# Grouped-query keys of x in one run of 512 columns: score matmuls 512 wide in a two-layer hybrid mixer

## Chip, cores and metric

The kernel runs on one core of a Trainium2 chip. The metric is device time in microseconds (us) of one execution, lower is better. All matrix products are made on TensorE (PE in the profile); VectorE is DVE, ScalarE is ACT, GpSimd is POOL, SyncE's queue of transfers is SP or SPq.

## The reference

Two layers of a mixer over 512 tokens of x and 256 tokens of a context. Each layer has three branches (differential attention, grouped-query attention, a long convolution). The change touches the second:

```python
def _gqa_attend(q, k, v):
    scale = GQ_DIM ** -0.5
    def body(qb):
        s = jnp.einsum('bqgrd,bkgd->bgrqk', qb, k).astype(jnp.float32) * scale
        p = jax.nn.softmax(s, axis=-1).astype(v.dtype)
        return jnp.einsum('bgrqk,bkgd->bqgrd', p, v)
    return _sweep_queries(body, q)
...
        kg_all = jnp.concatenate([kg_c, _rope_2d(kg, tab_gq)], axis=1)
        vg_all = jnp.concatenate([vg_c, vg], axis=1)
```

There are 8 query heads of 128 in 2 groups (g), each group with one key and one value head. Queries of x see all 768 keys (512 of x, 256 of the context). In the first layer the queries of the context see the 256 context keys alone; the second layer has no context output.

## The kernel before

Every fp32 operand is kept as a high part and a low part, and every product is three matmuls (`mm3`, lines 137 to 140: high by high, high by low, low by high) that add up in PSUM. A matmul has 128 stationary columns (a weight load, PEld, goes ahead of each) and streams 128, 256 or 512 columns of the other operand.

Tokens are worked on in pairs of 128-token tiles: pairs 0 and 1 are x, pair 2 is the context. For each group g the loop at lines 920 to 936 projects a pair (`proj_tok`, 48 matmuls of 256 columns into a PSUM tile `pst` of pool `pj`, which has two buffers), copies its value half out (`vv`, lines 927 and 582), norms and rotates its key half (`norm_rope`: products with tables at lines 598 and 602 read the same PSUM tile, a reciprocal root follows at lines 164 to 176), transposes the keys into another PSUM tile (line 932) and copies them out as a high and a low half of one SBUF tile `kk`. The dictionary `kT` has one such pair of 256 columns for each pair of tokens. These four places (two groups in two layers) are called the K stages below.

`scores` (lines 616 to 620) makes the scores of 128 queries: for each of the three pairs of keys one `mm3`, 256 columns into a part of a PSUM tile `S` of two banks of 512 columns. `softmax` takes the row maximum (DVE, line 634), the exponential (ACT, line 637) and the reciprocal; `pv` transposes the result (line 648) and multiplies it with the values (lines 655 to 658). `scores` is called with all three pairs 32 times in each layer, and in the first layer 16 times with the context pair alone.

The differential attention has its own scores (`scores_c`, lines 622 to 630, tiles `kH`, `kL`, `qT`), which the change leaves as they are. Its keys are taken from a projection by `evac_k` (lines 1037 to 1048), and its rotation products are at lines 1057 and 1061.

Attention steps, projections and the convolution's steps are generators that the projections tick, so the program mixes them. Then a scheduler puts each engine's instructions in order, from when it reckons that each can start. Engines run their own queues in order, and wait for each other by semaphores. All tiles named `u` (`vv`, `kk`, `qh`, the convolution's `uTh`, and others) share one pool of 20 buffers of 512 fp32 columns, handed out in the order of the program.

Of the kernel before, what the change touches and what calls it, by code (L numbers as in the profile page):

```python
# [11 lines left out]
F32R = mybir.dt.float32r  # L12
# [8 lines left out]
L, LC, D = 512, 256, 1024  # L21
# [47 lines left out]
def hybrid_mixer(ctx: ExitStack, tc: tile.TileContext, a, out):  # L69
# [5 lines left out]
    up = ctx.enter_context(tc.tile_pool(name="up", bufs=20))  # L75
# [61 lines left out]
    def mm3(ps, sh, sl, mh, ml, first, last):  # L137
        i0 = PE.matmul(ps, sh, mh, start=first, stop=False)  # L138
        PE.matmul(ps, sh, ml, start=False, stop=False)  # L139
        return i0, PE.matmul(ps, sl, mh, start=False, stop=last)  # L140
# [390 lines left out]
    def wchunk(l, ch):  # L531
        return [wload(a["w_in"][l, ch, :, 4 * j:4 * j + 4]) for j in range(2)]

    def layer(l, hx, hc, late, first):
# [7 lines left out]
        def proj_tok(W, pair):  # L542
            bg.tick()
            att.tock()
            ps = pj.tile([128, 2, 256], F32, tag="pj", name="pst")
            for i in range(2):
                for k in range(8):
                    Wh, Wl = W[k // 4]
                    mm3(ps[:, i], stat(2 * pair + i, k, 0), stat(2 * pair + i, k, 1),
                        Wh[:, k % 4], Wl[:, k % 4], k == 0, k == 7)  # L550
            return ps
# [16 lines left out]
        def gates(W, b0):  # L568
            for mb in range(2):
                for isx in ([True, False] if full else [True]):  # L570
                    n = L if isx else LC
                    ps = proj_feat(W, mb, isx)
                    v = tp.tile([128, n], F32, tag="tp", name="gv")
                    ACT.activation(v, ps, AF.Copy)
                    t = tp.tile([128, n], F32, tag="tp", name="sg")
                    sigmoid_into(t, v)
                    DVE.tensor_tensor(out=t, in0=v, in1=t, op=ALU.mult)
                    SP.dma_start(gd[12 * l + b0 + mb][:, 0:512] if isx else gd[12 * l + b0 + mb][:, 512:768], t)

        def evac_split(dh, dl, ps):  # L580
            ACT.activation(dh, ps, AF.Copy)  # L581
            return DVE.tensor_tensor(out=dl, in0=ps, in1=dh.bitcast(F32), op=ALU.subtract)  # L582

        def norm_rope(ps, H, pair, tab):
            g, C, S = tab
            v = ps.rearrange("p t (h d) -> p t h d", d=128)
            t1 = tp.tile([128, 2, H, 128], F32, tag="tp", name="t1")
            sq = tp.tile([128, 2, H, 128], F32, tag="tp", name="sq")
            ACT.activation(sq, v, AF.Square)
            if pair == 2:  # L590
                gb = g.unsqueeze(1).to_broadcast([128, H, 128])
                for t in range(2):
                    DVE.tensor_tensor(out=t1[:, t], in0=v[:, t], in1=gb, op=ALU.mult)
            else:
                t2 = tp.tile([128, 2, H, 128], F32, tag="tp", name="t2")
                for t in range(2):
                    tt = 2 * pair + t
                    DVE.tensor_tensor(out=t1[:, t], in0=v[:, t],
                                      in1=C[:, tt].unsqueeze(1).to_broadcast([128, H, 128]), op=ALU.mult)
                    for h in range(2):  # L600
                        d, s = slice(64 * h, 64 * h + 64), slice(64 - 64 * h, 128 - 64 * h)
                        DVE.tensor_tensor(out=t2[:, t, :, d], in0=v[:, t, :, s],  # L602
                                          in1=S[:, tt, d].unsqueeze(1).to_broadcast([128, H, 64]), op=ALU.mult)
                POOL.tensor_tensor(out=t1, in0=t1, in1=t2, op=ALU.add)
            ss = small(2 * H)
            DVE.tensor_reduce(out=ss, in_=sq.rearrange("p t h d -> p (t h) d"), axis=AX.X, op=ALU.add)
            r = rsqrt_cols(ss, 2 * H, 1.0 / 128)
            f = t1.rearrange("p t h d -> p (t h) d")
            DVE.tensor_tensor(out=f, in0=f, in1=r.unsqueeze(2).to_broadcast([128, 2 * H, 128]), op=ALU.mult)
            return f  # L610
# [4 lines left out]

        def scores(qh, ql, kT, klist):
            S = pS.tile([128, 1024], F32, tag="S", name="S")
            for i, kp in enumerate(klist):
                mm3(S[:, i * 256:(i + 1) * 256], qh, ql, kT[kp][0], kT[kp][1], True, True)
            return S  # L620

        def scores_c(c, q, kT, klist, i):
# [297 lines left out]
        for g in range(2):  # L920
            W = wchunk(l, GQ_C[g]["kv"])
            kT, V = {}, {}
            for p in pairs:
                ps = proj_tok(W, p)
                vv = up.tile([128, 2, 2, 128], F32R, tag="u", name="vv")
                vh, vl = vv[:, 0], vv[:, 1]
                evac_split(vh, vl, ps[:, :, 128:256])
                V[p] = (vh, vl)
                kr = norm_rope(ps[:, :, 0:128], 1, p, tabs["k"])
                T = pS.tile([128, 256], F32, tag="S", name="pst")  # L930
                for t in range(2):
                    PE.transpose(T[:, t * 128:(t + 1) * 128], kr[:, t], ident)
                kk = up.tile([128, 2, 256], F32R, tag="u", name="kk")
                kh, kl = kk[:, 0], kk[:, 1]
                evac_split(kh, kl, T)
                kT[p] = (kh, kl)
            for c in range(2):
                W = wchunk(l, GQ_C[g]["q"][c])
                qT = {}
                for p in qpairs:  # L940
                    ps = proj_tok(W, p)
                    qr = norm_rope(ps, 2, p, tabs["q"])
                    T = pS.tile([128, 2, 256], F32, tag="S", name="pst")
                    for h in range(2):
                        for t in range(2):
                            PE.transpose(T[:, h, t * 128:(t + 1) * 128], qr[:, 2 * t + h], ident)
                    qh = up.tile([128, 2, 256], F32R, tag="u", name="qh")
                    ql = up.tile([128, 2, 256], F32R, tag="u", name="ql")
                    evac_split(qh, ql, T)
                    qT[p] = (qh, ql)  # L950
                W = wchunk(l, GQ_C[g]["gate"][c])
                gates(W, 4 * g + 2 * c)
                if g == 0 and c == 0:
                    bg.drain()
                    for gen in late:
                        slow.add(gen)
                att.add(gq_att(g, c, kT, V, qT))
                att.spread(2 * len(qpairs) + 1, nq + {(0, 0): -full, (0, 1): 3, (1, 0): 0, (1, 1): 1}[g, c])
# [51 lines left out]
        for pr in range(2):  # L1010
# [10 lines left out]
            for hh in range(2):  # L1021
# [4 lines left out]
                qT, kT = {}, {}  # L1026
# [23 lines left out]
                for p in (0, 1):  # L1050
                    ps = proj_tok(W, p)
                    v = ps.rearrange("p t (c d) -> p t c d", d=64)
# [33 lines left out]
        def ysplit(i, src, shape):  # L1086
            if i < 12:
                t = hp.tile([128, 2] + shape, F32R, tag="h", name="yT")
            elif i < 14:
                t = dt.tile([128, 2] + shape, F32R, tag="dt", name="yT")  # L1090
            elif shape[0] == 1:
                t = up.tile([128, 2] + shape, F32R, tag="u", name="yT")
            else:
                t = None
            if t is not None:
                h, lo = t[:, 0], t[:, 1]
            else:
                h, lo = [pool.tile([128] + shape, F32R, tag=tag, name="yT")
                         for pool, tag in spare.get(i, [(up, "u")] * 2)]
            ACT.activation(h, src, AF.Copy)  # L1100
            (POOL if i < 12 else DVE).tensor_tensor(out=lo, in0=src, in1=h.bitcast(F32), op=ALU.subtract)
            return h, lo
# [13 lines left out]
        for b in order[8:15]:  # L1116
# [4 lines left out]
            if full and (b % 2 == 1 or b == 10):  # L1121
# [4 lines left out]
                h, lo = ysplit(ny, t, [len(bs), 256])  # L1126
# [228 lines left out]
    bg.add(f0)  # L1355
    bg.add(filter_gen(0, "0c", 256, h, w4))
    hx, hc = layer(0, hx, hc, [mod_gen(cs)], {b: (W0[b], acc[b]) for b in range(2)})
    bg.add(filter_gen(1, "1x", 512, h, []))
    layer(1, hx, hc, [], {})


# [137 lines left out]
```

## Time and profile before

| | us |
|---|---|
| median of 3 runs | 1585.81 (1583.59 to 1588.69) |
| the profiled execution, its own time | 1585.86 |
| its span, first to last instruction | 1584.1 |
| PE busy | 1500.6 (95%) |
| PE weight loads busy | 1349.7 (85%) |
| DVE busy | 1128.4 (71%) |
| ACT busy | 828.7 (52%) |
| POOL busy | 404.5 (26%) |

The span is 1.8 us shorter than the execution's own time. A matmul's shown duration includes its way through the array, and the next one starts before it ends: the durations of a run of matmuls add up to more than the time they take, and what one costs is the distance from its start to the next one's start.

### The profile page before, as it was taken

What the parts mean: (1) busy time and instruction counts of PE and PEld (TensorE: products, weight loads), DVE (VectorE), ACT (ScalarE), POOL (GpSimd) and SP (SyncE); (2) the same over time, 40 slices, a digit from 0 to 9 for tenths busy, and PEclk for the clock granted to TensorE, in tenths of its full rate; (3) what the DMA queues carried; (4) which work ended last, traced back from release to release, by engine and by line L of the source; (5) the groups of instructions that cost most, each with busy time, mean ns of one, the idle gap of its engine ahead of it and who ended that gap; (6) DMA issues with size and microseconds to landing.
All of it is one profiled execution on the core that took longest, in us unless ns stands there. A gap on an engine that the chain in (4) does not pass through costs nothing. (4 is left out here: it accounts for less than half of the span.)

```text
span 1584.1 us, 27024 instructions
## 1 busy us (share of the span) xinstructions
PE 1500.6 (95%) x10166; PEld 1349.7 (85%) x10166; DVE 1128.4 (71%) x2168; ACT 828.7 (52%) x1611; POOL 404.5 (26%) x436
## 2 busy tenths in 40 slices
PE   5989999999999999998999999998999999898997
PEld 3768888999998989898888878888999998798885
DVE  6767777877767475877754588769887656768657
ACT  5544343555466465666653356324556555657633
POOL 0243433212222141212002124233322223214014
PEclk9999999999999999999999999999999999999999
DMA  9437666323425253315343444764422222116242
GB/s 347 140 121 252 213 206 202 121 88 110 150 94 158 94 157 121 114 48 183 117 141 132 137 142 154 244 210 143 139 64 88 87 97 87 57 48 209 60 157 80
DMA packets 102134, 218.30 MB, mean 138 GB/s; under 512 B 11377, under 2 KB 46131, under 8 KB 102004
## 3 DMA queue, kind: packets, MB, share of 16 engines
q1 hardware_dynamic: 91492, 180.14, 34.6%
q0 software_dynamic: 9936, 35.39, 7.2%
q8 instruction: 80, 1.31, 0.3%
q10 hardware_dynamic: 576, 1.05, 0.2%
q14 instruction: 50, 0.41, 0.1%
HBM read 176.02 MB, written 40.52 MB: 137 GB/s over the span
## 5 line engine op out<-in xcount | busy, mean ns | idle before, releaser
L138 PE MATMUL psf<-hT,wh 128*128 128x512 f32 (+1 forms) x768 | 269.4, 355 | 13.5 <-DVE kL L1045 7.2
L138 PE MATMUL pst<-wh,hT 128*128 128x256 f32 x960 | 275.7, 287 | 6.7 <-DVE t L602 6.3
L140 PE MATMUL pst<-wh,hT 128*128 128x256 f32 x960 | 274.9, 286 | 0.0
L139 PE MATMUL pst<-wl,hT 128*128 128x256 f32 x960 | 274.4, 286 | 0.0
L139 PE MATMUL psf<-hT,wh 128*128 128x512 f32 (+1 forms) x768 | 268.3, 350 | 0.0
L140 PE MATMUL psf<-hT,wl 128*128 128x512 f32 (+1 forms) x768 | 267.6, 349 | 0.0
L156 DVE TENSOR_TENSOR wl<-raw,wh 128x1024 fp32r<-128x1024 f32 x140 | 178.2, 1274 | 93.2 <-ACT wh L152 82.9
L152 ACT ACTIVATE wh<-raw 128x1024 fp32r<-128x1024 f32 x140 | 147.9, 1057 | 94.5 <-PE psf L139 42.9
L138 PEld LDWEIGHTS pst<-wh,hT 128*128 128x128 f32 x960 | 184.4, 192 | 12.7 <-issue 10.0
L637 ACT ACTIVATE P<-S,sa 128x768 f32<-128x768 f32 (+1 forms) x160 | 130.2, 814 | 111.8 <-DVE sa L634 63.5
L139 PEld LDWEIGHTS pst<-wl,hT 128*128 128x128 f32 x960 | 184.5, 192 | 1.2 <-issue 0.8
L140 PEld LDWEIGHTS pst<-wh,hT 128*128 128x128 f32 x960 | 184.6, 192 | 0.9 <-issue 0.8
L138 PEld LDWEIGHTS psf<-hT,wh 128*128 128x128 f32 x768 | 146.2, 191 | 34.9 <-ACT P L977 4.3
L139 PEld LDWEIGHTS psf<-hT,wh 128*128 128x128 f32 x768 | 146.8, 191 | 16.7 <-issue 0.4
L140 PEld LDWEIGHTS psf<-hT,wl 128*128 128x128 f32 x768 | 146.4, 191 | 16.9
L634 DVE TENSOR_REDUCE sa<-S 128x1 f32<-128x768 f32 (+1 forms) x160 | 134.6, 841 | 26.9 <-PE S L629 17.7
L582 DVE TENSOR_TENSOR pl<-T,ph 128x512 fp32r<-128x512 f32 x156 | 107.0, 686 | 43.2 <-ACT ph L581 40.5
L581 ACT ACTIVATE ph<-T 128x512 fp32r<-128x512 f32 x156 | 92.6, 593 | 74.9 <-PE T L648 74.0
L138 PE MATMUL px<-wh,yT 128*128 128x512 f32 x320 | 126.1, 399 | 4.8 <-ACT P L977 3.6
L139 PE MATMUL px<-wl,yT 128*128 128x512 f32 x320 | 126.2, 395 | 0.0
L140 PE MATMUL px<-wh,yT 128*128 128x512 f32 x320 | 125.9, 394 | 0.0
L892 POOL TENSOR_TENSOR P<-P,sa 128x768 f32<-128x768 f32 (+1 forms) x40 | 52.4, 1309 | 207.6 <-DVE sa L639 198.1
(301 smaller groups left out, 3410.1 us busy)
## 6 DMA issues: line engine op xcount, KB each, us to landing
raw<-in_w_in SPq DMA_DIRECT2D x104, 512.0 KB, 4.1
raw<-in_w_out SPq DMA_DIRECT2D x36, 512.0 KB, 3.9
adaw<-in_ada_w SPq DMA_DIRECT2D x32, 512.0 KB, 4.6
tab<-in_inv POOLq DMA_DIRECT2D x20, 512.0 KB, 4.7
tab<-in_fwd POOLq DMA_DIRECT2D x18, 512.0 KB, 4.8
adaw<-in_ada SPq DMA_DIRECT2D x16, 512.0 KB, 10.6
yT<-yx POOLq DMA_DIRECT2D x16, 512.0 KB, 6.9
gl<-gd SPq DMA_DIRECT2D x60, 128.0 KB, 2.4
```

Of the source, the lines that this page charges most:

```text
L138: i0 = PE.matmul(ps, sh, mh, start=first, stop=False)
L139: PE.matmul(ps, sh, ml, start=False, stop=False)
L140: return i0, PE.matmul(ps, sl, mh, start=False, stop=last)
L152: ACT.activation(hi, src, AF.Copy)
L156: last_lo[0] = e.tensor_tensor(out=lo, in0=src, in1=hi.bitcast(F32), op=ALU.subtract)
L581: ACT.activation(dh, ps, AF.Copy)
L582: return DVE.tensor_tensor(out=dl, in0=ps, in1=dh.bitcast(F32), op=ALU.subtract)
L634: DVE.tensor_reduce(out=nm, in_=S[:, :n], axis=AX.X, op=ALU.max, negate=True)
L637: ACT.activation(P[:, :n], S[:, :n], AF.Exp, bias=nm, accum_out=s)
L892: POOL.tensor_tensor(out=P[:, :n], in0=P[:, :n], in1=rs.to_broadcast([128, n]), op=ALU.mult)
```

## The change

`kT` gets two entries for each group: `kT[True]`, a high tile `kkh` and a low tile `kkl` of 512 columns with all keys of x, and `kT[False]`, a tile `kk` with the two halves of the context's keys as before. Both 512-wide tiles are taken at pair 0 and each is written in two halves, by pair 0 and by pair 1. `scores` makes one `mm3` of 512 columns into the first bank of `S` and one of 256 into the second, in place of three of 256. The number of SBUF tiles is the same (three in each K stage); two of them are taken at pair 0.

```diff
         def scores(qh, ql, kT, klist):
             S = pS.tile([128, 1024], F32, tag="S", name="S")
-            for i, kp in enumerate(klist):
-                mm3(S[:, i * 256:(i + 1) * 256], qh, ql, kT[kp][0], kT[kp][1], True, True)
+            for isx, lo in [(True, 0), (False, 512)] if len(klist) > 1 else [(False, 0)]:
+                mm3(S[:, lo:lo + (L if isx else LC)], qh, ql, kT[isx][0], kT[isx][1], True, True)
             return S
...
-                kk = up.tile([128, 2, 256], F32R, tag="u", name="kk")
-                kh, kl = kk[:, 0], kk[:, 1]
-                evac_split(kh, kl, T)
-                kT[p] = (kh, kl)
+                if p == 0:
+                    kT[True] = [up.tile([128, 512], F32R, tag="u", name=nm) for nm in ("kkh", "kkl")]
+                if p < 2:
+                    evac_split(*[v[:, p * 256:(p + 1) * 256] for v in kT[True]], T)
+                else:
+                    kk = up.tile([128, 2, 256], F32R, tag="u", name="kk")
+                    kT[False] = (kk[:, 0], kk[:, 1])
+                    evac_split(*kT[False], T)
```

The scheduler also puts other instructions in another order, from the first K stage on (the lines after the K stage are numbered 4 higher). Three places follow.

PE, the scores of the first 128 queries (tile `S`, first layer, group 0), before:

```order
L138 MATMUL S_3622<-kk_2905,qh_3215 128x256
L139 MATMUL S_3622<-kk_2905,qh_3215 128x256
L140 MATMUL S_3622<-kk_2905,ql_3216 128x256
L138 MATMUL S_3622<-kk_3002,qh_3215 128x256
L139 MATMUL S_3622<-kk_3002,qh_3215 128x256
L140 MATMUL S_3622<-kk_3002,ql_3216 128x256
L138 MATMUL S_3622<-kk_3094,qh_3215 128x256
L139 MATMUL S_3622<-kk_3094,qh_3215 128x256
L140 MATMUL S_3622<-kk_3094,ql_3216 128x256
```

The same scores on PE in the changed kernel:

```order
L138 MATMUL S_3622<-kkh_2905,qh_3215 128x512
L139 MATMUL S_3622<-kkl_2906,qh_3215 128x512
L140 MATMUL S_3622<-kkh_2905,ql_3216 128x512
L138 MATMUL S_3622<-kk_3094,qh_3215 128x256
L139 MATMUL S_3622<-kk_3094,qh_3215 128x256
L140 MATMUL S_3622<-kk_3094,ql_3216 128x256
```

Nine matmuls of 256 columns become three of 512 and three of 256. In the whole program the matmuls on `S` from these keys go from 624 to 432.

DVE, the K stage of the first layer's group 0, where pair 1's projection (`pst_2922`, in the changed kernel `pst_2923`) is read, before (`us` is the convolution's, `wl` the low part of weights, `vv_2971` pair 1's values):

```order
L582 TENSOR_TENSOR uTl_2919<-uT_2915,uTh_2918 128x256
L582 TENSOR_TENSOR vv_2971<-pst_2922,vv_2971 128x256
L156 TENSOR_TENSOR wl_3443<-raw_3440,wh_3442 128x1024
L598 TENSOR_TENSOR t1_2974<-pst_2922,Ck_2789 128x128
L602 TENSOR_TENSOR t2_2977<-pst_2922,Sk_2790 128x64 x2
L598 TENSOR_TENSOR t1_2974<-pst_2922,Ck_2789 128x128
L602 TENSOR_TENSOR t2_2977<-pst_2922,Sk_2790 128x64 x2
L606 TENSOR_REDUCE sm_2985<-sq_2975 128x2
L778 SCALAR_TENSOR_TENSOR us_2809<-yps_2604,rn0x_1280,us_2809 128x256 x2
```

The same stretch of DVE's queue in the changed kernel:

```order
L582 TENSOR_TENSOR uTl_2920<-uT_2916,uTh_2919 128x256
L156 TENSOR_TENSOR wl_3443<-raw_3440,wh_3442 128x1024
L582 TENSOR_TENSOR vv_2972<-pst_2923,vv_2972 128x256
L582 TENSOR_TENSOR vv_3069<-pst_3020,vv_3069 128x256
L778 SCALAR_TENSOR_TENSOR us_2809<-yps_2604,rn0x_1280,us_2809 128x256 x2
L598 TENSOR_TENSOR t1_2975<-pst_2923,Ck_2789 128x128
L602 TENSOR_TENSOR t2_2978<-pst_2923,Sk_2790 128x64 x2
L598 TENSOR_TENSOR t1_2975<-pst_2923,Ck_2789 128x128
L602 TENSOR_TENSOR t2_2978<-pst_2923,Sk_2790 128x64 x2
```

Pair 2's values (`vv_3069`) and the convolution's two `us` instructions now stand ahead of the last reads of pair 1's projection.

DVE, differential attention of the last head of the first layer, where the keys of pair 0 (`kL_9325`, in the changed kernel `kL_9229`) are read out of their projection, before:

```order
L1033 SCALAR_TENSOR_TENSOR qT_9320<-pst_9260,qT_9320 64x256 x2
L1057 TENSOR_TENSOR t1_9504<-pst_9455,cosD_990 128x512
L639 RECIPROCAL sa_9254<-sa_9252 128x1
L1061 TENSOR_TENSOR t2_9505<-pst_9455,sinD_992 128x8x32 x2
L976 TENSOR_TENSOR sa_9256<-sa_9254,nl0_973 128x1
L634 TENSOR_REDUCE sa_9340<-S_9333 128x1
L1045 TENSOR_TENSOR kL_9325<-pst_9260,kH_9324 64x256 x2
```

The same stretch of DVE's queue in the changed kernel:

```order
L1037 SCALAR_TENSOR_TENSOR qT_9224<-pst_9164,qT_9224 64x256 x2
L639 RECIPROCAL sa_9158<-sa_9156 128x1
L980 TENSOR_TENSOR sa_9160<-sa_9158,nl0_973 128x1
L1049 TENSOR_TENSOR kL_9229<-pst_9164,kH_9228 64x256 x2
L1050 CAST kH_9228<-kH_9228 64x256
L634 TENSOR_REDUCE sa_9244<-S_9237 128x1
L1061 TENSOR_TENSOR t1_9408<-pst_9359,cosD_990 128x512
L1065 TENSOR_TENSOR t2_9409<-pst_9359,sinD_992 128x8x32 x2
```

The read of the keys now stands ahead of the row maximum and of the other pair's rotation products.

## Rows read from the trace of the kernel before

**Rows 1.** The page, part 1: busy time, share and instructions.

```profile
PE 1500.6 (95%) x10166; PEld 1349.7 (85%) x10166; DVE 1128.4 (71%) x2168; ACT 828.7 (52%) x1611; POOL 404.5 (26%) x436
```

**Rows 2.** Busy time by stretch: bounds, length, PE, PEld, DVE, ACT, POOL, clock, DMA.

```profile
260.00:300.00 40.00, 36.57 (x274) 35.38 (x273) 33.70 (x87) 15.92 (x35) 13.25 (x11) 0.96 0.47 155
300.00:640.00 340.00, 338.09 (x2549) 309.14 (x2548) 228.70 (x485) 189.72 (x404) 79.21 (x89) 1.00 0.39 123
1130.00:1340.00 210.00, 207.13 (x1536) 196.65 (x1537) 150.65 (x300) 123.17 (x237) 51.22 (x54) 1.00 0.28 90
```

**Rows 3.** PE's groups by line and shape: busy us, mean ns of one, idle before.

```profile
L139 PE MATMUL psf<-hT,wh 128*128 128x512 f32 x448 | 177.0, 395 | 0.0
...
L138 PE MATMUL S<-kk,qh 128*128 128x256 f32 x208 | 61.4, 295 | 0.5 <-ACT P L637 0.5
```

**Rows 4.** Timeline of PE, the first 18 score matmuls and the next: start, duration.

```profile
309.85 0.28 PE L138 MATMUL S<-kk,qh 128*128 128x256 f32 x1
...
312.01 0.28 PE L138 MATMUL pst<-wh,hT 128*128 128x256 f32 x1
```

**Rows 5.** Timeline of PE, 13 matmuls of 512 columns, first and last.

```profile
301.06 0.39 PE L140 MATMUL psf<-hT,wl 128*128 128x512 f32 x1
...
303.79 0.39 PE L140 MATMUL psf<-hT,wl 128*128 128x512 f32 x1
```

**Rows 6.** Timeline of the K stage, first layer, group 0, all engines.

```profile
263.21 0.28 PE L140 MATMUL pst<-wh,hT 128*128 128x256 f32 x1
...
263.41 1.06 ACT L152 ACTIVATE wh<-raw 128x1024 fp32r<-128x1024 f32 x1
...
263.96 0.42 DVE L582 TENSOR_TENSOR uTl<-uT,uTh 128x256 fp32r<-128x256 f32 x1
...
264.30 0.42 DVE L582 TENSOR_TENSOR vv<-pst,vv 128x256 fp32r<-128x256 f32 x1
264.63 1.22 DVE L156 TENSOR_TENSOR wl<-raw,wh 128x1024 fp32r<-128x1024 f32 x1
264.69 2.58 POOL L773 TENSOR_SCALAR us<-us,cols 128x512 f32<-128x512 f32 x1 [2.24 <-DMA us<-hyu]
...
265.76 0.28 DVE L598 TENSOR_TENSOR t<-pst,Ck 128x128 f32<-128x128 f32 x1
...
266.42 0.34 DVE L602 TENSOR_TENSOR t<-pst,Sk 128x64 f32<-128x64 f32 x2
...
266.91 0.39 PE L138 MATMUL pst<-wh,hT 128*128 128x256 f32 x1 [3.43 <-DVE t L602]
...
267.31 0.88 DVE L778 SCALAR_TENSOR_TENSOR us<-yps,rn0x,us 128x256 f32<-128x256 f32 x2 [0.22 <-POOL us L773]
```

**Rows 7.** Timeline of PE: two other long waits.

```profile
745.28 0.55 PE L138 MATMUL psf<-hT,wh 128*128 128x256 f32 x1 [4.15 <-DVE kL L1045]
...
1074.08 0.35 PE L138 MATMUL pst<-wh,hT 128*128 128x256 f32 x1 [2.85 <-DVE t L602]
```

**Rows 8.** Timeline of DVE and ACT ahead of the wait that ends at 745.28.

```profile
739.64 0.69 DVE L1057 TENSOR_TENSOR t<-pst,cosD 128x512 f32<-128x512 f32 x1
739.82 0.60 ACT L1042 ACTIVATE kH<-pst 128x512 fp32r<-128x512 f32 x1
740.32 0.73 DVE L1061 TENSOR_TENSOR t<-pst,sinD 128x256 f32<-128x256 f32 x2
740.97 2.53 DVE L976 TENSOR_TENSOR sa<-sa,nl 128x1 f32<-128x1 f32 x1
743.42 0.94 DVE L634 TENSOR_REDUCE sa<-S 128x1 f32<-128x768 f32 x1
744.29 0.84 DVE L1045 TENSOR_TENSOR kL<-pst,kH 64x256 fp32r<-64x256 f32 x2
```

**Rows 9.** Busy time by stretch, right behind two of the waits; the clock follows POOL.

```profile
267.10:270.50 3.40, 3.40 (x17) 3.40 (x17) 3.16 (x8) 1.04 (x3) 1.67 (x3) 0.50 0.54 186
745.00:748.40 3.40, 3.12 (x15) 3.15 (x15) 3.08 (x6) 1.71 (x4) 0.00 (x0) 0.50 1.13 418
```

## The prediction

> **What bounds the kernel now.** I read the page's busy line first [rows 1]: PE is busy for 95% of the span, DVE for 71%, so what the change saves on PE should count, unless it falls into a wait. The table by stretch says where: between 300 and 640 us and between 1130 and 1340 us, where nearly all the scores of grouped-query attention are made, PE is busy 338.09 of 340 us and 207.13 of 210 us [rows 2]. There is no idle time there for a saving to vanish in. In the K stage between 260 and 300 us PE is busy 36.57 of 40 [rows 2], and one wait explains that: 3.43 us, ended by DVE's last read of a projection [rows 6].
>
> The groups by line come next, and they are easily misread. A matmul of 512 columns is shown with a mean of 395 ns, one of 256 columns with 295 [rows 3]. From these, two narrow ones made into one would save about 195 ns. But shown durations overlap, and what counts is the distance between starts. The timeline shows 18 score matmuls of 256 columns from 309.85 to 312.01 [rows 4]: 2.16 us, 120 ns each. It shows twelve distances of 512-column matmuls from 301.06 to 303.79 [rows 5]: 2.73 us, 227 ns each. So 256 more columns cost 227 - 120 = 107 ns, and a matmul has 120 - 107 = 13 ns that do not depend on its columns.
>
> **Term 1, fewer matmuls.** 64 calls of `scores` with all keys (32 in each layer) lose three matmuls each: 624 become 432, 192 fewer, with the same number of columns. Each pair merged saves 2 x 120 - 227 = 13 ns on PE: 192 x 13 = 2.5 us. The weight loads that go with them (also 192 fewer) are already hidden, since 120 ns is the distance with one load for each matmul. Bounds: 0, if the 13 ns were columns after all, and 192 x 120 = 23.0 us, if the second half of a wide matmul cost nothing. Twelve equal distances of 227 ns put it at 13 ns.
>
> The Trainium skill (TensorE: Matmul & The Clock Gate, Back-to-back issue gap) gives two other figures. Its formula for a lone matmul has a fixed cost of 2.5 ns; by that the sum would have 192 x 2.5 = 0.5 us here in place of 2.5. Its sustained figure for 512 columns is about 131 ns, by which 192 x (240 - 131) = 20.9 us would go, an estimate from that page. This case's timeline agrees with neither: 13 ns and 227 ns [rows 4, 5].
>
> DVE's row maximum, ACT's exponential, the transposes, the bytes of keys copied out and all DMAs are the same in number and size. The two copies of each pair's keys go into halves of other tiles, at no cost. The first scores stand at 309.85 [rows 4], long after the K stage's copies, so waiting for both halves delays nothing; without that cover a copy of 0.42 us, like that of `vv` [rows 6], would show in each K stage.
>
> **Term 2, the K stage of the first layer.** The 20 `u` buffers are handed out in program order. Two buffers for keys are now taken at pair 0, so pair 2's values no longer stand behind pair 1's keys, and DVE gets them earlier: ahead of its last reads of pair 1's projection. PE waits for just these reads at 266.91, because the next projection needs that PSUM buffer [rows 6]. I replay DVE's new order with the durations of before. `uTl` ends at 264.38 (263.96 + 0.42). Then `wl` (1.22) ends at 265.60, two copies of values (0.42 each) at 266.44. The two `us` instructions now stand next; they need POOL's product, which ends at 264.69 + 2.58 = 267.27, and take 0.88: 268.15. The reads of the projection took from 265.76 to 266.76 (266.42 + 0.34), 1.00 us: 269.15. PE started 0.15 us after the last one and now would at 269.30: 2.4 us later. Queued behind these on DVE is the rest of pair 1's rotation, and for that PE waits only after another 48 matmuls (5.8 us at 120 ns). ACT's copy of the weights from 263.41 to 264.47 [rows 6] is moved ahead of pair 1's values, which DVE reaches later still. The SP and POOL queues have the same order up to here, so the transfer that POOL waits for is not moved. Bounds: 0, if POOL has its input 2.4 us sooner or DVE is earlier by another wait that shortens, and 4.0 us: the 2.4, and the clock. Right behind this wait the granted clock is 0.50 for 3.4 us [rows 9], the lower of TensorE's two levels, 1.2 in place of 2.4 GHz: in 745.00 to 748.40, after the other such wait, 15 matmuls of 256 columns ran, where 28 would fit at 120 ns, so such a stretch costs 13 x 120 ns = 1.6 us. A longer wait could bring a second one. I take 2.4, since the reads' order leaves the `us` instructions no way round.
>
> **Term 3, the last head of the first layer.** PE waits 4.15 us up to 745.28 for DVE's read of the keys `kL` [rows 7]. Ahead of it on DVE stand a 128x1 product of 2.53 us, stretched while POOL works, and a row maximum of 0.94 [rows 8]. In the new order the row maximum and the other pair's two rotation products (0.69 and 0.73) stand behind `kL`; so do, with the latter, the POOL additions that need them. Bounds: 0.94, the row maximum alone, and 4.15 + 1.6 = 5.8, the whole wait with the slow stretch after it [rows 9]; ACT's copy `kH` is there at 740.42 [rows 8], so `kL` could be. What is late next is the other pair's rotation, by 0.69 + 0.73 = 1.4 us, and PE's transposes wait for it. I take 4.15 - 1.4 = 2.7 us.
>
> Elsewhere the scheduler moves instructions by a few places on all engines, and waits shrink and grow. I find no side for that and take 0, with some 3 us to either side: about the size of one wait like that at 1074.08 [rows 7].
>
> **Sum**, against the profiled execution's own 1585.86 us (the median of three runs is 1585.81, the same): 1585.86 - 2.5 + 2.4 - 2.7 = 1583.1 us, 0.2% faster. About 0.3% (4.8 us) is what a measurement of this kernel can tell from no change.
>
> **Rivals.**
> - *Faster: the waits go too.* Term 3 at its far end (5.8), term 2 at 0: 1585.86 - 2.5 - 5.8 = 1577.6. For it: a wait of over 3 us with a slow clock behind it is worth more than the whole of term 1, and the new order undoes its cause at 745. Against: the same order lengthens the one at 266.91.
> - *Slower: values ahead of rotation.* In each of the four K stages DVE takes pair 2's values before pair 1's or the queries' rotation products, and PE waits for a PSUM buffer: 4 x 2.4 = 9.6, and the wait before 1074.08, of 2.85 us, behind which the first matmul took 0.35 us and not 0.55 as at 745.28 [rows 7], becomes long enough for one slow stretch: 1585.86 - 2.5 + 9.6 + 1.6 = 1594.6. It decides from (4.8 + 2.5) / 4 = 1.8 us for each stage. Against: the second group's stages showed no such wait before, with other work for PE to do, and the second layer's first has no `us` instruction in that place.
> - *Only columns count.* The change saves no PE time at all; terms 2 and 3 alone: 1585.86 + 2.4 - 2.7 = 1585.6. Against: 227 is not 240.
> - *Wide matmuls overlap.* The far end of term 1: 1585.86 - 23.0 + 2.4 - 2.7 = 1562.6. Against: [rows 5]. The page's 131 ns would give 1564.7, an estimate; the trace disagrees.
>
> **How the numbers follow.** Forecast (1583.1, within 0.3%) 0.50; only columns 0.05, also within; the waits go 0.31; wide matmuls overlap 0.01; slower 0.13. That is faster 0.32, same 0.55, slower 0.13. The forecast's own range is 3 us to either side for the moved waits and 1.6 for a slow stretch: 1578.5 to 1587.7. The range that should hold 8 in 10 reaches down to the faster rival, 1577, and up to where two of the four K stages are longer by 2.4 with a slow stretch and without term 3: 1585.86 - 2.5 + 4.8 + 1.6 = 1589.8, so 1590. What is left out is most of the slower rival and a tail of the faster one.
>
> **What would show it.** Term 1: 64 matmuls of 512 columns on `S` from each line of `mm3`, 227 ns from start to start, and a pair of score blocks taking 6 x 227 + 6 x 120 ns = 2.08 us in place of 2.16. Term 2: PE's wait near 267 us at 5 to 6 us, ended again by line 602. Term 3: the wait near 740 us ended by `kL` under 2 us. Wrong it would be if PE's idle time in the K stages or in differential attention changed by more than 3 us in a direction not named here, or if wide score matmuls stood further apart than 227 ns.

## The result and the profile after

The changed kernel takes 1596.35 us (median of 6 runs, 1595.01 to 1599.08); the kernel before took 1587.57 us beside it (6 runs). The ratio is 1.0054 with a 95% interval of 1.0041 to 1.0068: 0.5% slower, some 8.6 us. The forecast was 0.2% faster, with a range that ended at 1590. The profiled execution took 1599.08 us, with a span of 1597.0.

The page's busy line after, to be read beside [rows 1]:

```profile
PE 1508.8 (94%) x9974; PEld 1348.1 (84%) x9974; DVE 1120.5 (70%) x2168; ACT 826.1 (52%) x1611; POOL 406.1 (25%) x436
```

192 matmuls and weight loads are gone, as counted. The same three stretches as in [rows 2]:

```profile
260.00:300.00 40.00, 34.70 (x260) 34.01 (x259) 32.80 (x83) 14.13 (x32) 13.92 (x12) 0.91 0.43 135
300.00:640.00 340.00, 338.22 (x2458) 306.59 (x2457) 227.56 (x489) 188.50 (x401) 78.48 (x88) 1.00 0.38 121
1130.00:1340.00 210.00, 207.25 (x1439) 191.93 (x1438) 149.06 (x301) 120.20 (x231) 53.81 (x51) 1.00 0.28 91
```

In the two long stretches PE is as full as it was. In the K stage it lost 1.87 us of work (36.57 to 34.70), and the granted clock fell from 0.96 to 0.91.

PE's timeline of a pair of score blocks, first matmuls of each and the one behind them (for [rows 4]):

```profile
315.39 0.40 PE L138 MATMUL S<-kkh,qh 128*128 128x512 f32 x1
...
316.44 0.40 PE L138 MATMUL S<-kkh,qh 128*128 128x512 f32 x1
...
317.49 0.28 PE L138 MATMUL pst<-wh,hT 128*128 128x256 f32 x1
```

A pair takes 317.49 - 315.39 = 2.10 us in place of 2.16; 2.08 was forecast. The medians of the distances behind the 64 wide score matmuls of each line are 234, 232 and 229 ns for lines 138, 139 and 140, a little over the 227 of [rows 5]. Term 1 is there, at 32 x 0.06 = 1.9 us.

The K stage of the first layer, all engines, for [rows 6]:

```profile
264.36 1.06 ACT L152 ACTIVATE wh<-raw 128x1024 fp32r<-128x1024 f32 x1 [0.98 <-PE pst L139]
...
265.45 1.23 DVE L156 TENSOR_TENSOR wl<-raw,wh 128x1024 fp32r<-128x1024 f32 x1 [1.75 <-ACT wh L152]
...
266.20 1.05 ACT L152 ACTIVATE wh<-raw 128x1024 fp32r<-128x1024 f32 x1
...
267.15 0.65 ACT L581 ACTIVATE vv<-pst 128x256 fp32r<-128x256 f32 x2
267.28 1.62 DVE L156 TENSOR_TENSOR wl<-raw,wh 128x1024 fp32r<-128x1024 f32 x1 [0.27 <-ACT wh L152]
268.82 0.74 DVE L582 TENSOR_TENSOR vv<-pst,vv 128x256 fp32r<-128x256 f32 x2
269.27 0.76 ACT L589 ACTIVATE sq<-pst 128x256 f32<-128x256 f32 x2 [1.47 <-DVE vv L582]
269.49 0.86 DVE L778 SCALAR_TENSOR_TENSOR us<-yps,rn0x,us 128x256 f32<-128x256 f32 x2
...
270.93 0.34 DVE L602 TENSOR_TENSOR t<-pst,Sk 128x64 f32<-128x64 f32 x2
...
271.42 0.55 PE L138 MATMUL pst<-wh,hT 128*128 128x256 f32 x1 [5.30 <-DVE t L602]
```

The wait of 3.43 us has become 5.30, ended by line 602 as forecast. The reader should follow the chain backward: the reads stand behind both `us`, these behind two copies of values, and those behind the split of the weights, which waits for ACT's `wh`. ACT copies the values (267.15) behind `wh` (266.20), where it did so ahead of it before.

The end of the first layer, all engines, where the wait of 4.15 us for `kL` stood [rows 7, 8]:

```profile
753.52 0.68 DVE L1105 TENSOR_TENSOR yT<-yld,yT 128x512 fp32r<-128x512 f32 x1
...
754.22 0.80 SPq L1122 DMA_DIRECT2D yld<-yx  x2
...
757.78 0.63 ACT L1104 ACTIVATE yT<-yld 128x512 fp32r<-128x512 f32 x1 [2.37 <-DMA yld<-yx]
758.32 0.58 ACT L1034 ACTIVATE qT<-pst 128x512 fp32r<-128x512 f32 x1
758.80 0.92 ACT L981 ACTIVATE P<-P,sa 128x768 f32<-128x768 f32 x1
759.62 0.59 ACT L581 ACTIVATE ph<-T 128x512 fp32r<-128x512 f32 x1
...
760.26 0.39 PE L655 MATMUL O<-ph,vh 128*128 128x256 f32 x1 [3.40 <-ACT ph L581]
```

The wait for `kL` is gone. A new one of 3.40 us, for `ph`, stands 15 us later. ACT's `ph` is behind `yT`, and `yT` waits 2.37 us for a load that SyncE issued only at 754.22, when DVE's subtraction from the last load's buffer (753.52 + 0.68 = 754.20) had set it free.

The table by stretch, 6.8 us each at these two waits (for [rows 9]):

```profile
270.20:277.00 6.80, 5.58 (x26) 5.62 (x27) 5.62 (x21) 1.34 (x5) 2.00 (x2) 0.50 0.48 151
761.80:768.60 6.80, 6.06 (x26) 5.66 (x27) 5.08 (x12) 4.53 (x8) 0.92 (x2) 0.50 0.12 35
```

At both the clock is at its lower level, 1.2 GHz, for 6.8 us, where it was 3.4 before. The first stretch begins 1.2 us before PE starts again, the second 1.5 us after.

### The profile page after: what moved, and what is told of

It reads as the page before. It is cut to its first block, busy times and chain, and to the rows that moved or that the text cites. A ratio compares the mean times of both kernels' runs of the same rounds, so it can differ in the third digit from the quotient of the medians.

```text
span 1597.0 us, 26656 instructions
## 1 busy us (share of the span) xinstructions
PE 1508.8 (94%) x9974; PEld 1348.1 (84%) x9974; DVE 1120.5 (70%) x2168; ACT 826.1 (52%) x1611; POOL 406.1 (25%) x436
## 3 DMA queue, kind: packets, MB, share of 16 engines
q10 hardware_dynamic: 576, 1.05, 0.2%
```

## The experiments

**Change and order taken apart (e1, e2).** The scheduler that orders the instructions also moved hundreds of others. So I fixed the order. `_in_this_order` ties each instruction to the one ahead of it in a list for its engine, on all five engines, and adds no wait between engines.

e1, the changed kernel in the order before:

```diff
         hybrid_mixer(tc, args, out)
+        _in_this_order(tc, nc)    # lists of the kernel before
```

> The changed kernel's tiles and its 512-column score matmuls, with every engine's instructions in the order of the kernel before (the two matmuls of 256 columns of a pass become the one of 512 in the place of the first). Theory A, the order makes the loss: the time is the kernel before's less what 192 fewer matmuls save, 1587.6 - 2 = 1585.6 us, ratio 0.9987, and the two waits of the key stages for the reads of line 602 are 3.4 and 2.9 us as before. Rival B, the wide matmuls themselves make it (longer rows, a lower granted clock): about the changed kernel's 1596 us, ratio 1.005, with twice the stretches at half clock.

Measured: 1585.94 us, ratio 0.9986 (0.9971 to 1.0002). PE's timeline:

```profile
267.75 0.35 PE L138 MATMUL pst<-wh,hT 128*128 128x256 f32 x1 [3.42 <-DVE t L602]
...
744.85 0.55 PE L138 MATMUL psf<-hT,wh 128*128 128x256 f32 x1 [4.17 <-DVE kL L1049]
...
1074.72 0.55 PE L138 MATMUL pst<-wh,hT 128*128 128x256 f32 x1 [2.85 <-DVE t L602]
```

All three long waits are back at their old size. The kernel before with its own order tied in the same way was not run, so what tying alone does is not shown apart; e2 below, tied, takes as long as the changed kernel, which is not.

e2, the changed kernel's order with narrow matmuls:

```diff
-                mm3(S[:, lo:lo + (L if isx else LC)], qh, ql, kT[isx][0], kT[isx][1], True, True)
...
+                mm3(S[:, i * 256:(i + 1) * 256], qh, ql, kh, kl, True, True)   # halves of kT[True]
...
+        _in_this_order(tc, nc)    # lists of the changed kernel
```

> The changed kernel's tiles with score matmuls of 256 columns, with every engine's instructions in the order of the changed kernel (each pass over x is two matmuls of 256 where the one of 512 stood). Theory A, the order makes the loss: the changed kernel's time plus about 2 us for 192 more matmuls, 1598 us, ratio to the kernel before 1.0065. Rival B, the wide matmuls make it: the kernel before's time, 1587.6 us, ratio 1.000.

Measured: 1595.56 us, ratio 1.0052 (1.0036 to 1.0069). Its long waits in the first layer are those of the changed kernel, in PE's timeline:

```profile
271.73 0.55 PE L138 MATMUL pst<-wh,hT 128*128 128x256 f32 x1 [5.79 <-DVE t L602]
...
760.27 0.38 PE L656 MATMUL O<-ph,vh 128*128 128x256 f32 x1 [2.77 <-ACT ph L581]
```

Theory A holds: the order makes the loss, and the wide matmuls do no harm. In the order before they save 2.2 us (0.14%), in the new order nothing that shows (1.0054 beside 1.0052); the intervals are as wide as the effect, and e1's does not exclude that they save nothing.

**Which part of the change moves the order (e3, e4).** e3 keeps the keys in one run but makes narrow matmuls, in the scheduler's own order:

```diff
-                mm3(S[:, lo:lo + (L if isx else LC)], qh, ql, kT[isx][0], kT[isx][1], True, True)
...
+                mm3(S[:, i * 256:(i + 1) * 256], qh, ql, kh, kl, True, True)   # halves of kT[True]
```

> Only the tiles of the change: keys of x in one run of 512 per half, score matmuls of 256 columns over its two halves, in the order that the scheduler gives by itself. In its key stages the values of pair 2 and the convolution's us stand ahead of the reads of pair 1's projection as in the changed kernel; most of the rest stands as in the kernel before. If the order of the key stages makes the loss (3 us in each of two): 1593.6 us, ratio 1.004. If the order elsewhere makes it: 1588 to 1590, ratio 1.001. Rival B, wide matmuls: 1587.6, ratio 1.000.

Measured: 1590.23 us, ratio 1.0018 (1.0005 to 1.0032), between the two. The first layer's K stage has the longer wait, the second layer's has not:

```profile
271.46 0.55 PE L138 MATMUL pst<-wh,hT 128*128 128x256 f32 x1 [5.19 <-DVE t L602]
...
1078.56 0.55 PE L138 MATMUL pst<-wh,hT 128*128 128x256 f32 x1 [2.84 <-DVE t L602]
```

The wait of 4.16 us for `kL` is still there, at 750.12. So the run of keys by itself moves the first layer's K stage, at some 3 us. The rest moves only with the wide matmuls in the scheduler's plan, which are fewer and have other durations.

e4 ties only pair 2's values, which the prediction blamed together with `us`:

```diff
+                with (tc.issue_after(khi.ins) if p else ExitStack()):   # khi: ACT's copy of the keys before
                     evac_split(vh, vl, ps[:, :, 128:256])
```

> The changed kernel with one tie more: ScalarE's copy of a pair's values is issued behind its copy of the keys of the pair before, so that the values of pair 2 no longer stand ahead of pair 1's rotation on VectorE. If the values' place in the key stages makes the loss: 1596.4 - 6 = 1590 us, ratio 1.0015, with the waits for line 602 back at about 3.4 and 2.9 us. If it is made by the order elsewhere, or by the wide matmuls: about 1596 us, ratio 1.005.

Measured: 1595.16 us, ratio 1.0045 (1.0032 to 1.0059), a miss. DVE and PE in the timeline (lines are numbered one higher here):

```profile
269.53 0.88 DVE L779 SCALAR_TENSOR_TENSOR us<-yps,rn0x,us 128x256 f32<-128x256 f32 x2 [1.13 <-POOL us L774]
...
271.47 0.55 PE L138 MATMUL pst<-wh,hT 128*128 128x256 f32 x1 [5.79 <-DVE t L603]
```

The values are gone from that place, but the two `us` still stand ahead of the reads, and DVE waits 1.13 us for POOL's product there. Without the values it only waits longer.

**Where the order costs (e5, e6, e7).** The two orders have the same instructions behind them at about 405 us and at the layers' border, so they can be joined there. Each kernel is the changed one with lists of both; only this differs:

```diff
+        _in_this_order(tc, nc)    # e5: new order up to 405 us, then before's
+        _in_this_order(tc, nc)    # e6: new order from 405 us to the end of layer 0
+        _in_this_order(tc, nc)    # e7: new order in layer 1
```

> The changed kernel (wide matmuls) with its own order of instructions up to 405 us, the key stage of the first layer with it, and the kernel before's order from there on. From e1 (1585.9, all in the order before): if the key stage costs what the offsets between the traces say, 2.4 us of longer wait and 1.7 us of one more stretch at half clock, 1585.9 + 4.1 = 1590.0 us, ratio 1.0013. Rival, the loss belongs to the order elsewhere and the wait is made good within the heads: 1586, ratio 0.9988.

> The changed kernel with its own order only from 405 us to the end of the first layer; the first 405 us and the second layer in the order before. The offsets between the traces grow by 3 us in that stretch: 1585.9 + 3 = 1589 us, ratio 1.0007, with the wait of 4.2 us for kL near 745 gone and one for ph near 760 in its place. Rival, that growth was drift between two single executions: 1586, ratio 0.9988.

> The changed kernel with its own order in the second layer and the order before in the first. The offsets between the traces grow by 4 us there: 1585.9 + 4 = 1590 us, ratio 1.0012. Rival, the second layer's loss only follows from the first layer's (a later start of the loads): 1586, ratio 0.9988. The three gains of e5, e6 and this one should add up to the 10.4 us between e1 and the changed kernel.

Measured: e5 1589.70 us, ratio 1.0014 (1.0001 to 1.0028); e6 1593.94, 1.0030 (1.0013 to 1.0046); e7 1588.81, 1.0005 (0.9993 to 1.0017). Over e1's 0.9986 that is 0.28%, 0.44% and 0.19%: 4.4, 7.0 and 3.0 us. The sum, 14.4, is more than the 10.8 between e1 and the changed kernel (0.68%); with some 3 us of uncertainty in each that is no contradiction, but the third share alone is not certain to differ from nothing. The middle one is the largest, and twice what the offsets between two traces had led me to expect.

The traces, one execution each, place the loss more narrowly. VectorE runs 2168 instructions in each of these kernels, and at its 351st, 617th, 1231st, 1474th and 2131st it has the same ones behind it in both orders. The time from one to the next, in us (e9 to e11, below, are listed where they keep the new order):

| VectorE's instructions | order before | new order |
|---|---|---|
| 351st to 617th, up to 405 us | 150.3, 150.6, 150.6 (e1, e6, e7) | 152.8, 152.4, 153.4 (changed, e5, e10) |
| 617th to 1231st, the rest of the first layer | 445.2, 446.2, 445.5 (e1, e5, e7) | 448.4, 449.1, 447.7 (changed, e6, e9) |
| 1474th to 2131st, second layer | 486.8, 486.8, 485.9 (e1, e5, e6) | 488.5, 488.3, 487.6, 488.1, 487.4 (changed, e7, e9, e10, e11) |

The two groups do not overlap in any row. By their means the new order costs 2.4, 2.8 and 1.5 us, 6.7 in all, less than the medians give. Between the traces of e1 and of the changed kernel lie 11.5 us: 7.4 in these three stretches, 1.3 in the second layer's K stage, and 2.8 where the order is the same.

That K stage has the same order on VectorE in all of them: the two lists of the second layer differ only behind its reads. Its wait is longer in some executions even so. First e6, then e7, SyncE's queue, POOL, DVE and PE in the timeline:

```profile
1066.54 0.38 SPq L772 DMA_DIRECT2D sg<-hyg  x1
...
1071.37 1.30 POOL L790 TENSOR_TENSOR accH<-accH,sq 128x512 f32<-128x512 f32 x1
...
1071.43 1.80 DVE L792 SCALAR_TENSOR_TENSOR y<-us,cols,sg 128x512 f32<-128x512 f32 x1 [2.60 <-DMA sg<-hyg]
...
1080.60 0.55 PE L138 MATMUL pst<-wh,hT 128*128 128x256 f32 x1 [4.12 <-DVE t L602]
```

```profile
1064.26 0.38 SPq L772 DMA_DIRECT2D sg<-hyg  x1
...
1067.78 0.75 DVE L792 SCALAR_TENSOR_TENSOR y<-us,cols,sg 128x512 f32<-128x512 f32 x1 [1.24 <-DMA sg<-hyg]
...
1077.04 0.36 PE L138 MATMUL pst<-wh,hT 128*128 128x256 f32 x1 [2.85 <-DVE t L602]
```

The longer wait goes with a load. DVE's line 792 starts when `sg` is there, 4.9 us after the issue in e6 and 3.5 us in e7. In e6 it then lies beside GpSimd's product and takes 1.80 us in place of 0.75: 1.05 us more, where the two waits are 1.27 apart. All fourteen traces fall into these two kinds. In eight (the changed kernel, where the wait is 4.13 at 1084.52, e4, e6 and e8 to e12) line 792 starts 4.6 to 5.2 us after the issue and takes 1.5 to 2.1 us; in the six others 3.0 to 3.7 us, and it takes 0.75. Why the load takes longer in some stays open.

**Two places put back (e9, e10, e11).** All three are the changed kernel with its own lists, but for a few instructions. e9 edits the K stage near 267 us:

```diff
 ACT
-wh 2nd half, vv pair 1, vv pair 2, sq pair 1
+vv pair 1, wh 2nd half, sq pair 1, vv pair 2
 DVE
-wl 2nd half, vv pair 1, vv pair 2, us x2, reads of pair 1 (598, 602)
+vv pair 1, wl 2nd half, reads of pair 1 (598, 602), vv pair 2, us x2
```

> The changed kernel in its own order but for the first layer's key stage, near 267 us: ScalarE's copy of pair 1's values stands ahead of its copy of the second half of the next weights, and on VectorE the split of pair 1's values ahead of that of those weights, and the reads of lines 598 and 602 ahead of pair 2's values and the convolution's us, as in the kernel before. If these places make the longer wait, it falls from 5.3 to about 3.4 us and one stretch at half clock goes: 1596.4 - 1.9 - 1.7 = 1592.8 us, ratio 1.0032. Rival, the wait is set by the later arrival of the weights and comes back behind them: 1596, ratio 1.0052.

e10 edits the end of the layer near 758 us:

```diff
 ACT
-yT (1104), qT, P (981), ph, P (637)
+qT, P (981), ph, P (637), yT (1104)
 DVE
-yT (1105), qT x2, P (982), pl
+qT x2, P (982), pl, yT (1105)
```

> The changed kernel in its own order but for one load near 758 us: ScalarE's copy into yT (line 1104), which waits 2.4 us for a load, and VectorE's subtraction behind it (line 1105) stand behind the four instructions of the last heads that followed them. If that copy blocks the heads, the wait of 3.4 us for ph falls to about 1 and the stretch at half clock behind it shortens: 1596.4 - 2.4 - 1.7 = 1592.3 us, ratio 1.0030. Rival, the heads wait there for their own softmax anyway: 1596, ratio 1.0052.

e11 has both edits:

> Both edits of e9 and e10 at once. If both hold and add up: 1596.4 - 3.6 - 4.1 = 1588.7 us, ratio 1.0008, about the kernel before. If the loss is spread over many small waits of the heads, most of it stays: 1594 to 1596, ratio 1.004 to 1.005.

Measured: e9 1593.08 us, ratio 1.0030 (1.0016 to 1.0043); e10 1591.46, 1.0018 (1.0006 to 1.0031); e11 1588.21, 0.9998 (0.9988 to 1.0008). From the changed kernel's 1.0054 these are 3.8, 5.7 and 8.9 us, beside the 3.6, 4.1 and 7.7 expected. PE's timeline at the two places, e9 and then e10:

```profile
269.80 0.55 PE L138 MATMUL pst<-wh,hT 128*128 128x256 f32 x1 [3.73 <-DVE t L602]
```

```profile
757.60 0.38 PE L655 MATMUL O<-ph,vh 128*128 128x256 f32 x1 [0.61 <-ACT ph L581]
```

The wait for `ph` falls from 3.40 us to 0.61, and that in the K stage from 5.30 to 3.73. In e10 the stretch at the lower clock behind it is gone too; in e9 the one behind the K stage still lasts 6.8 us, which its expectation had shorter. The table by stretch of e10, 6.8 us behind 757.60:

```profile
757.60:764.40 6.80, 5.70 (x40) 4.95 (x41) 6.21 (x14) 5.50 (x11) 1.28 (x3) 1.00 0.77 266
```

On VectorE the rest of the first layer (617th to 1231st instruction) takes 443.3 us in e10 and 442.8 in e11: 5.4 less than in the new order, and 2.6 less than in the order before. Up to 405 us e9 and e11 take 152.5 and 151.8, only 0.7 less than the new order; the rest of e9's 3.8 us is not found there, and its interval is some 3 us to either side.

In the places that were edited stand 25 of the program's 14,334 instructions; moved by a few places, they take back 8.9 of the 10.8 us.

**A version faster than both (e8, e12).** e8 takes the order before with wide matmuls and puts DVE's reads of PSUM first:

```diff
 DVE, first layer's K stage; in the second layer's also ahead of a product of line 754
-wl, reads of pair 1 (598, 602)
+reads of pair 1 (598, 602), wl
 DVE, 740 us
-sa (980), P's maximum (634), kL x2 (1049)
+kL x2 (1049), sa (980), P's maximum (634)
```

> The wide matmuls in the order before, with three edits on VectorE alone: the reads of pair 1's projection (lines 598 and 602) ahead of the split of the next weights (line 156) in both layers' key stages, and the two subtractions into kL (line 1049) ahead of the product of line 980 that stood 2.55 us beside three products of GpSimd near 740 us. Waits of 3.4, 2.9 and 4.2 us should fall to about 2.2, 1.2 and 0.8: 6.1 us, and up to 1.7 us for each of the stretches at half clock that follow them. 1585.9 - 6 = 1580 us, ratio 0.995, at best 1576. Rival: the next split, or the head behind the product of line 980, becomes the wait, and the time stays at 1585 to 1586.

Measured: 1583.99 us, ratio 0.9983 (0.9967 to 0.9999). It gained 0.5 us over e1, of 6 expected. PE's timeline:

```profile
266.18 0.55 PE L138 MATMUL pst<-wh,hT 128*128 128x256 f32 x1 [2.83 <-DVE t L602]
...
1069.12 0.35 PE L138 MATMUL pst<-wh,hT 128*128 128x256 f32 x1 [2.41 <-DVE t L602]
...
1077.61 0.41 PE L932 MATMUL pst<-ident,t 128*128 128x128 f32 x2 [2.50 <-DVE t L609]
```

In the first layer the reads first gave 0.6 us, since they then wait for ACT's square (line 589). In the second layer the wait is 2.41 us. It has the late load, with which the others wait 4.1, so the gain there is nearer 1.7 than 0.4; but a new wait of 2.50 us took more than that back. e12 leaves the second layer's edit out:

> e8 without its edit in the second layer, where a wait of 2.5 us for line 609 took the place of the one that fell: the wide matmuls in the order before, the first layer's reads ahead of the next split, and the two subtractions into kL ahead of the product of line 980. From e1's 0.9986 the gains of 0.6 and 2.6 us that e8's trace showed at these places: 1582.7 us, ratio 0.9966. Rival: what a wait gives here comes back at the next one, as in e8: 1584 to 1586, ratio 0.998 to 0.9986.

Measured: 1582.49 us, ratio 0.9962 (0.9947 to 0.9978), 0.4% faster than before. In its timeline PE waits 0.82 us for `kL` at 742.02, where it was 4.15. What e12 has over e1 (0.24%, 3.8 us) is about as wide as the intervals. The traces bear it out: VectorE's 617th to 1231st instruction take 442.5 us in e12 and 442.1 in e8, 3.3 less than in the order before.

## Why the prediction was wrong

**Term 1 held.** 192 fewer matmuls, 2.10 us a pair, and 2.2 us in e1 beside the 2.5 forecast, though by its interval e1 alone could be nothing. *Only columns count* and *Wide matmuls overlap* are out by the distances of 229 to 234 ns. These are over the 227 that the prediction named as a sign of being wrong. Its twelve "equal" distances ran from 226 to 233; the part that does not depend on columns is nearer 10 ns than 13, by 0.06 us for the six matmuls that a pair loses.

**Term 2 had the right place, and by the traces the right size.** The wait was forecast at 5.8 us and came at 5.30, and at 5.2 to 5.8 in e2 to e5. The price I took, 2.4 us, is what the stretch up to 405 us costs on VectorE, by the means. The medians put it higher, at 4.4 (e5) and 3.8 (e9), with some 3 us of uncertainty in each; e5 also has a wait of 1.85 us at 416.55, some 10 us behind the joint, which neither e1 nor the changed kernel has. The second stretch of slow clock came: 6.8 us at 0.50. The `us` ahead of the reads hold them up as forecast. In e2, e4, e5 and e10, where the wait is 5.79 or 5.80, they wait 0.8 to 1.1 us for POOL's product; in the changed kernel and e3 (5.30 and 5.19) the product is ready, and they stand behind the values alone.

The stated reason was wrong. With the two buffers taken at pair 0 but the keys kept apart, the scheduler's list is the order before on ACT and DVE (that kernel was not run); with the keys merged and narrow matmuls (e3), it gives the longer wait. So it is not that two buffers for keys are taken at pair 0. It is rather that pair 1's keys need none of their own, so pair 2's values no longer queue behind them; that is argued, not shown. Pair 2's values alone, which I blamed with `us`, can be moved off without any gain (e4). e9's edits were made together, so the single shares of ACT's copy behind `wh`, the values and `us` stay open.

**Term 3 is the step that failed.** The wait for `kL` did go, as it said. But "what is late next is the other pair's rotation, by 0.69 + 0.73 = 1.4 us" was wrong: next was ACT's copy into `yT`, which stood waiting for a load ahead of the last heads' `ph`. I had followed the new order on DVE to the next PE wait and had not read ACT's order there, nor asked when its load could be issued. In place of a gain of 2.7 us, the new order of this stretch costs 2.8 us by the traces. By e6's median it costs 7.0, with the second layer's longer wait of 1.3 us in its trace. The copy moved back takes off 5.4 us by the traces and 5.7 by e10's median. What is left is then 2.6 us shorter than in the order before: the forecast gain was there, and the copy hid it. That the size agrees so closely is luck in part, since the new order has other waits that term 3 did not name (in e11 1.33 us for POOL's line 1068 at 710.43, and for `kL` 1.05 at 658.38, where e1 has 0.69). Between the forecast, 2.8 us faster, and the measurement, 8.6 slower, lie 11.4 us; term 3 makes 5.5 of them by the traces and 9.7 by the medians.

**Elsewhere 0, some 3 us to either side.** The second layer's new order cost 3.0 us by e7's median, which by its interval could be nothing, and 1.5 by the traces. Added up, -1.9 + 2.4 + 2.8 + 1.5 = 4.8 us of the 8.6 are placed by the traces; the rest stays open.

**The rivals.** *Slower: values ahead of rotation* gave 1594.6, near the time measured, but its mechanism did not happen: one K stage of four became longer by its order. The second layer's longer wait comes and goes with one load (e6, e7). That its number was near is luck. The range was too narrow upward because I let term 3 only shrink, never turn its sign.

## What to carry to other kernels

When a scheduler writes the order, a change of one tile is two changes: the work, and a new order for everything. Run the new work in the old order and the old work in the new; here that took two runs, and showed a loss of some 10 us from the order alone and, under it, a gain of about 2, no larger than the noise. Before counting a wait as gone, read what every engine does in the next 15 us of the new order, the loads' issue included: an in-order engine that waits for a load holds up all that stands behind it. Putting reads of PSUM that TensorE waits for ahead of other VectorE work paid for `kL` (e12); in e8's second layer the next wait took it back, so each such move wants its own run.

## What was not expected of the hardware

A product of 128x1 on DVE takes 0.16 us, but 2.53 in [rows 8]. In e12 it stood at 741.90, DVE and then POOL in the timeline:

```profile
741.03 0.85 DVE L1049 TENSOR_TENSOR kL<-pst,kH 64x256 fp32r<-64x256 f32 x2
741.90 1.70 DVE L980 TENSOR_TENSOR sa<-sa,nl 128x1 f32<-128x1 f32 x1
743.63 0.96 DVE L634 TENSOR_REDUCE sa<-S 128x1 f32<-128x768 f32 x1
```

```profile
741.43 0.77 POOL L1068 TENSOR_TENSOR t<-t,t 128x256 f32<-128x256 f32 x1
742.11 0.78 POOL L1002 TENSOR_TENSOR y<-y,sq 128x256 f32<-128x256 f32 x1
742.80 0.77 POOL L1068 TENSOR_TENSOR t<-t,t 128x256 f32<-128x256 f32 x1
```

It ends when GpSimd's run of three products ends (742.80 + 0.77 = 743.57), while `kL`, which reads PSUM, took its usual 0.85 beside the first. I went through all 2168 instructions of DVE in the trace before: 80 are more than 0.4 us longer than the median of their kind. All 80 have their operands in SBUF alone and lie beside an instruction of GpSimd; of the some 1000 that read PSUM, none is among them. The changed kernel has 72 such, again none that reads PSUM. The Trainium skill (SBUF — State Buffer, Who interferes with whom) says that DVE shares one pair of SBUF ports with GpSimd, that a DVE instruction with two SBUF inputs contends for it with a GpSimd instruction that reads SBUF, and that whoever comes first has the pair for its whole instruction while the other is blocked. The trace agrees for this product, and shows it held up for several instructions in a row.

The length at the lower clock behind one and the same wait is not fixed: 3.4 us behind 3.43 us in the kernel before [rows 9], 6.8 behind 3.73 in e9, 3.4 behind 3.84 in e6. What decides between them stays open, and with it about 1.7 us of each term that ends in such a stretch.
